# Gate and up products: hi and lo of the activations side by side as one 512-column operand

## The chip, the cores and the metric

The kernel runs on one core of a Trainium2 chip, as one launch. The metric is the device time of that launch in microseconds (us); smaller is better. Engines are named as the profile names them: PE is TensorE (its weight loads are listed apart as PEld), ACT is ScalarE, DVE is VectorE, POOL is GpSimd, and SP issues the transfers.

## The reference, cut to what matters

The program is a two-layer decoder trunk on 256 tokens of 1024 features in float32: four SwiGLU half steps, an attention and convolution mixer between the first and second of them, and an RWKV-7 mixer between the third and fourth. The change is about the half steps:

```python
def macaron_half_ffn(x, pre_g, post_g, w_gate, w_up, w_down):
    h = rmsnorm(x, pre_g)
    h = (jax.nn.silu(h @ w_gate) * (h @ w_up)) @ w_down
    return x + 0.5 * rmsnorm(h, post_g)
```

`w_gate` and `w_up` are 1024 x 2816, `w_down` is 2816 x 1024.

## The kernel before

**Products.** A float32 number is split into two parts, hi and lo, whose sum it is, both of type float32r. A product is three matmuls into one bank of PSUM: hi by hi, hi by lo and lo by hi. `mm3` (L257) issues them, at L260, L261 and L262; its argument `a` is the operand that is loaded as weights (128 x 128), `b` the one that streams past them. `split_u` (L206) makes the two parts of a piece of weights: hi on ACT (L219), lo on DVE, and for every third piece in a half step on POOL (L224).

**Activations.** `norm_in` (L178) allocates two tiles, hi and lo, each of 8 blocks of 128 features by 256 tokens. `pre_norm` scales a tile of 128 tokens, and `hT_split` (L296) transposes it and splits it into the two tiles.

**A half step** (`ffn_body`, L390) has three parts.
- The first 512 of the 2816 columns, in token layout (L402 to L422): the activations are the loaded operand, 512 columns of weights stream.
- The other 2304 columns, transposed (L424 to L439). One round of the loop on `kb` takes 256 columns of gate and 256 of up, 9 rounds in all. Here 128 columns of weights (8 blocks of 128 x 128) are the loaded operand, called a set below, and the 256 tokens stream. A bank holds two sets beside each other, 256 columns each: one `fl` bank for gate, one `mm` bank for up. A set takes 8 calls of `mm3`. Behind a round stand Silu of the gate bank (ACT, L436), its product with the up bank (DVE, L437), and the split of the result into hi and lo (ACT L203, DVE L204). This part is called the wide stage.
- `out_proj` (L329): the product with `w_down`, 512 columns of weights streaming, into two `fl` and two `mm` banks, and behind it the norm and the sum with x.

**Order of work.** Transfers of 1 MB into four `raw` buffers are issued by SP in the order of the program. A set's hi and lo each take one of 18 `u` buffers, so about nine sets of weights can be ready; the split of a set further on waits until PE has finished a set. PSUM has two `fl` banks, four `mm` banks and two for transposes. A scheduler orders the instructions of each engine when the program is built; each engine then runs its own list in order.

Of the kernel before, what the change touches and what calls it, by code (L numbers as in the profile page):

```python
# [15 lines left out]
P = 128  # L16
D = 1024
S = 256
# [11 lines left out]
class Trunk:  # L30
    # out_proj: steps of a tile-1 tail ahead of the next part's first transposes; its last k blocks go by halves
    PIN = 15
    LAST = 4
    # the weight piece behind which the second tile of x is loaded
    LEAD = (0, 4)
    # layer 0: every how many splits Pool takes one
    SHQ = 2
    SH0 = 2
    # order of work for the tensor engine: c compressed branch, f other projections, m masks; a attention, f convolution
    PROJ = "fccfccccfcccmmfcmcfmmffcfcmfmfcmffcfffccmmmmffccc"  # L40
    ATT = "ffafaffafaffaaaafffaafffaafaaafaaafaafffaaafafafaffaffafffaafafafaafffaaafaaaafffffaffaafa"
# [7 lines left out]
    # columns of the forward substitution's groups  # L49
    CA = 6  # L50
    CB = 11
    # beside the substitution: b bonus, t tokens, v values, h g gates, z zeros
    FILL = "vvvz-vvtvvvbvvvhth-vvvvtthvtvtvv-h-vv-h-"
    # behind it: 0-3 chunks, a-d their norms, x y 64 x 64 inverses, A B gains, p q outputs, o the projection
    TAIL = ("vvvgvz0xxvxx0A00gAggsB0eA000aAy1a1y1a1aa1yBy11b1bb2B22b2B2b222ocpocc33cc33p3d/3dooddodqooo"
            "ooooooq")
    # chunks whose squares are summed on DVE; (chunk, half) scaled on ACT; (tile, half) of the outputs on Pool
# [25 lines left out]
    # ---- storage  # L83
# [24 lines left out]
    def behind(self, engine):  # L108
        """what is traced inside goes behind all that is traced so far on engine"""
        traced = self.nc.cur_bb.bb.instructions  # L110
        return self.tc.issue_after(next(i for i in reversed(traced) if i.engine == engine))

    @contextmanager
    def pe_after(self, ins):
        """the matmuls traced inside wait for ins"""
        traced = self.nc.cur_bb.bb.instructions
        n = len(traced)
        yield
        for i in traced[n:]:
            if i.engine == mybir.EngineType.PE:  # L120
                self.tc.add_manual_dep(i, ins.ins.name, mybir.DependencyInfo(
                    mybir.DependencyClass.Sync, mybir.DependencyReason.DATA))

    @contextmanager
    def pe_in_order(self):
        """the matmuls traced inside are issued as they are traced"""
# [11 lines left out]
    def paced(self, main, fill):  # L138
        """fill in step with main, each of its steps behind the instruction that main yields"""
# [5 lines left out]
    def packed(self):  # L145
        """a carver of small pieces out of one tile of a mixer"""
# [22 lines left out]
    def gain_cols(self, name):  # L169
        """a gain by features on partitions, [128, 8], from a small transfer"""  # L170
# [6 lines left out]

    def norm_in(self, gname):  # L178
        """-> (hi, lo, start): start(m) norms token tile m of x, transposes and splits it"""
        hilo = []  # L180

        def start(m, first=False):
            if m < 0:
                hilo.extend([(self.gain_cols if first else self.gain)(gname), self.b8k(F32R), self.b8k(F32R)])
                return
            g, hi, lo = hilo
            if g.shape[1] == KD:
                self.hT_split(self.pre_norm(m), hi, lo, m, g)
            else:
                self.hT_split(self.pre_norm(m, g), hi, lo, m)  # L190
# [10 lines left out]
    # ---- weights: float32 pieces split exactly into hi + lo, both float32r  # L201
# [4 lines left out]
    def split_u(self, src):  # L206
# [3 lines left out]
        if n == 1 and src.shape[2] == 512:  # L210
            # the first weights: every third piece on the two other engines
# [15 lines left out]
    def load_w(self, src, nk, pieces, transfers=1):  # L227
        """src [128, nk, cols]: split in `pieces` pieces along k; per k (hi, lo)"""
# [11 lines left out]
    def cols(self, src, spans):  # L240
        """the given (start, width) column spans of src [128, 8, cols], side by side"""
# [15 lines left out]
    def mm3(self, out, a, b, start, stop):  # L257
        """out += a^T b, a = (hi, lo), b = (hi, lo)"""
# [5 lines left out]
    # ---- norms  # L264
# [23 lines left out]
    def transposed(self, src, n):  # L288
        """n blocks of 128 columns of src -> [128, n, 128] in PSUM"""
# [6 lines left out]
    def hT_split(self, xn, hi, lo, m, g=None):  # L296
        for h in range(2):
            pt = self.transposed(xn[:, h * 512:(h + 1) * 512], 4)
            s = (slice(None), slice(h * 4, h * 4 + 4), slice(m * P, (m + 1) * P))
            if g is None:  # L300
                self.split(pt, hi[s], lo[s])
                continue
            for i in range(4):
                k = h * 4 + i
                s = (slice(None), k, slice(m * P, (m + 1) * P))
                self.nc.scalar.activation(hi[s], pt[:, i, :], AF.Copy, scale=g[:, k:k + 1])
                self.nc.vector.scalar_tensor_tensor(lo[s], pt[:, i, :], g[:, k:k + 1], hi[s].bitcast(F32),
                                                    op0=ALU.mult, op1=ALU.subtract)

    def post_norm(self, m, g, half):  # L310
        """x[m] += c * rmsnorm(y) * g, y coming in two halves"""
# [16 lines left out]
    # ---- x += c * rmsnorm(a^T w): tile 0 ahead of tile 1 from the k block `split` on  # L328
# [56 lines left out]
    # ---- SwiGLU half step  # L385
    def ffn(self, p):
        hilo, start = self.norm_in(p + "_pre_g")
        return start, lambda after: self.ffn_body(p, *hilo[1:], after)

    def ffn_body(self, p, hhi, hlo, after):  # L390
# [5 lines left out]
        def h(k, m):  # L396
            return hhi[:, k, m * P:(m + 1) * P], hlo[:, k, m * P:(m + 1) * P]
# [4 lines left out]
        # first 512 columns in token layout, tile 0 ahead of tile 1  # L402
# [20 lines left out]
        # the others transposed, both tiles at once  # L423
        for kb in range(4, KF, 2):  # L424
            if kb % 8 == 0:
                at.append((self.b8k(F32R), self.b8k(F32R)))
            bg, bu = self.fbank(), self.bank()
            for src, b in ((wg, bg), (wu, bu)):
                raw = self.cols(src, [(kb * P, 2 * P)])
                for i in range(2):  # L430
                    w = self.split_cols(raw, i * P, P)
                    for k in range(KD):
                        self.mm3(b[:, i * S:(i + 1) * S], w[k], (hhi[:, k, :], hlo[:, k, :]), k == 0, k == KD - 1)
            t = self.xn()
            sg, aa = t[:, :512], t[:, 512:]
            nc.scalar.activation(sg, bg, AF.Silu)  # L436
            nc.vector.tensor_mul(aa, bu, sg)  # L437
# [5 lines left out]
    # ---- layer 0 mixer: sparse attention heads beside a gated short convolution  # L443
    def l0_mix(self):
        hilo, start = self.norm_in("l0_mix_pre_g")
        return start, lambda after: self.l0_body(*hilo[1:], after)

    def l0_body(self, hhi, hlo, after):
# [11 lines left out]
        def h(k, m):  # L460
            return hhi[:, k, m * P:(m + 1) * P], hlo[:, k, m * P:(m + 1) * P]

        def hh(k):
            return hhi[:, k, :], hlo[:, k, :]

        def gather(b, pairs):
            """b = sum of the products, in steps of two"""
# [5 lines left out]
        # queries (scaled, transposed, heads r and r + 4 stacked) and values in token layout  # L473
# [12 lines left out]
        kcT = pk(2, NB)   # the two groups beside each other, each in its own rows  # L486
# [5 lines left out]
        # values and gates side by side  # L492
# [31 lines left out]
        # and the gates, 1 + exp(-g)  # L524
# [15 lines left out]
        # distances, ALiBi and masks  # L540
# [18 lines left out]
        # block features: (parity, dim) on partitions, so that 16 products of 128 rows cover a block  # L559
# [79 lines left out]
        def combine(m, i, ob):  # L639
            """oa[m] += gate_i / sum_i * branch output"""  # L640
# [10 lines left out]
        # selected blocks (all of them at these shapes), window (wider than the sequence)  # L651
# [142 lines left out]
    # ---- layer 1 mixer: RWKV-7 in four chunks of 64 tokens  # L794
# [10 lines left out]
    def l1_setup(self, st):  # L805
# [3 lines left out]
        # per-channel vectors as columns  # L809
# [14 lines left out]
        # first halves of the low-rank maps: decay and rate side by side, and the same times mu  # L824
# [10 lines left out]
    def l1_mixin(self, st, out, i, k, t0, n):  # L835
        """out = h + (shifted h - h) * mu_i for channel block k, tokens t0 .. t0 + n"""
# [3 lines left out]
    def l1_vraw(self, st, hh, i):  # L840
        """value weights, columns of half hh, channel blocks 4 i .. 4 i + 3"""
# [26 lines left out]
    def l1_body(self, st, after):  # L868
# [13 lines left out]
        # constants  # L882
        ones = pk(1)
        V.memset(ones, 1.0)
        mask = pk(P)      # strictly later | not earlier, the same for both halves of the rows
# [4 lines left out]
        rst = pk(CH * 65)  # a running sum that starts over every chunk  # L890
        V.memset(rst, 1.0)
        V.memset(rst[:, 0:CH * 65:65], 0.0)
        sel = self.small.tile([P, NC, 16], F32R, name="sel")   # head of a channel
# [18 lines left out]
        # values: token layout, centred per head (the head norm takes the mean out again);  # L912
        # ZV has the chunk's state updates in rows 0..63 and its values in rows 64..127
# [45 lines left out]
        BK = lambda c: gk[c // 4][:, c % 4]     # [128, chunk, b | k]  # L959
        KR = lambda c: kr_[c // 4][:, c % 4]    # [128, chunk, kappa | r]  # L960
# [16 lines left out]
        # low-rank maps, second halves  # L977
# [29 lines left out]
        def mixes():  # L1007
            """the other mixed inputs, a few blocks at a time"""
# [30 lines left out]
        # keys, decays and in-context rates, two heads at a time  # L1039
# [40 lines left out]
        hsp = self.b8(F32R).rearrange("p (a b s) -> p a b s", a=2, b=2)   # odd | even blocks, hi | lo  # L1080
# [12 lines left out]
        def gram(c):  # L1093
            """per head and chunk: (b | k) against (kappa | r), rows the earlier token"""
# [33 lines left out]
        # head sums -> per token: 1 / |k|^2 and the bonus  # L1128
# [23 lines left out]
        def base():  # L1152
            """inverses of the 32 x 32 diagonal blocks of I + diag(rn) A, one block of one head per partition"""
# [10 lines left out]
            # forward substitution in three independent groups of columns  # L1164
# [19 lines left out]
        def spread(g):  # L1184
            """the inverted blocks of chunks 2 g, 2 g + 1 to the rows of their tokens"""
# [9 lines left out]
        def x64(g):  # L1195
            """the corner blocks of the transposed 64 x 64 inverses"""
# [291 lines left out]
```

## Time and profile before

| | us |
|---|---|
| time, three runs | 1176.79, 1180.26, 1182.51 |
| median | 1180.26 |
| profiled execution, span from first to last instruction | 1176.0 |
| PE busy in the span | 1120.0 |
| PE weight loads busy | 994.9 |
| DVE, ACT, POOL busy | 651.8, 553.3, 441.0 |
| wide stage of one half step (four in all) | about 104 |

The page gives the profiled execution by its span alone. The span lies 0.8 us under the lowest of the three times and 4.3 us under their median, so the profiled execution is like the fastest of the runs. Matmuls are pipelined, and a matmul's record lasts longer than the distance to the next one's start; the rate of PE is therefore read from the distances between starts in the timeline, not from the duration of a record. A row of a group ends with the time its engine sat idle before such instructions and what ended that; idle time of an engine that nobody waits for costs nothing.

### The profile page before, as it was taken

What the parts mean: (1) busy time and instruction counts of PE and PEld (TensorE: products, weight loads), DVE (VectorE), ACT (ScalarE), POOL (GpSimd) and SP (SyncE); (2) the same over time, 40 slices, a digit from 0 to 9 for tenths busy, and PEclk for the clock granted to TensorE, in tenths of its full rate; (3) what the DMA queues carried; (4) which work ended last, traced back from release to release, by engine and by line L of the source; (5) the groups of instructions that cost most, each with busy time, mean ns of one, the idle gap of its engine ahead of it and who ended that gap; (6) DMA issues with size and microseconds to landing.
All of it is one profiled execution on the core that took longest, in us unless ns stands there. A gap on an engine that the chain in (4) does not pass through costs nothing. (4 is left out here: it accounts for less than half of the span.)

```text
span 1176.0 us, 18835 instructions
## 1 busy us (share of the span) xinstructions
PE 1120.0 (95%) x7581; PEld 994.9 (85%) x7581; DVE 651.8 (55%) x1021; ACT 553.3 (47%) x962; POOL 441.0 (37%) x400
## 2 busy tenths in 40 slices
PE   7999998998989999998999999988889988999997
PEld 5999986898978999887999988776557866999986
DVE  5543425656876444327543434879883786544431
ACT  6544434245755444435544432557543455544430
POOL 3523233232564323224523343434461654432321
PEclk9999999989999999999999999999996889999999
DMA  9955562542556665545765552532312244855520
GB/s 322 286 179 179 183 206 67 161 144 72 175 174 206 199 200 189 181 145 179 228 202 162 181 179 90 176 113 72 108 44 83 73 138 149 251 180 181 178 108 36
DMA packets 130756, 187.59 MB, mean 160 GB/s; under 512 B 6871, under 2 KB 101087, under 8 KB 130670
## 3 DMA queue, kind: packets, MB, share of 16 engines
q1 hardware_dynamic: 130670, 186.41, 48.9%
q8 instruction: 59, 0.97, 0.3%
q14 instruction: 27, 0.22, 0.1%
HBM read 185.34 MB, written 1.05 MB: 158 GB/s over the span
## 5 line engine op out<-in xcount | busy, mean ns | idle before, releaser
L224 POOL TENSOR_TENSOR u<-raw,u 128x512 fp32r<-128x512 f32 x222 | 317.3, 1451 | 495.9 <-ACT u L219 477.8
L219 ACT ACTIVATE u<-raw 128x1024 fp32r<-128x1024 f32 x312 | 328.1, 1058 | 338.8 <-PE mm L261 162.4
L224 DVE TENSOR_TENSOR u<-raw,u 128x1024 fp32r<-128x1024 f32 x201 | 273.8, 1366 | 267.1 <-ACT u L219 266.6
L260 PE MATMUL fl<-b,u 128*128 128x256 f32 x688 | 198.0, 288 | 0.1
L262 PE MATMUL fl<-b,u 128*128 128x256 f32 x688 | 197.6, 287 | 0.0
L261 PE MATMUL fl<-b,u 128*128 128x256 f32 x688 | 196.6, 286 | 0.0
L261 PE MATMUL mm<-b,u 128*128 128x256 f32 x592 | 167.7, 283 | 0.0
L262 PE MATMUL mm<-b,u 128*128 128x256 f32 x592 | 167.6, 283 | 0.0
L260 PE MATMUL mm<-b,u 128*128 128x256 f32 x592 | 167.6, 283 | 0.0
L260 PEld LDWEIGHTS fl<-b,u 128*128 128x128 f32 x688 | 133.7, 194 | 1.1 <-ACT u L219 0.5
L262 PEld LDWEIGHTS fl<-b,u 128*128 128x128 f32 x688 | 133.6, 194 | 0.8 <-POOL u L224 0.2
L261 PEld LDWEIGHTS fl<-b,u 128*128 128x128 f32 x688 | 133.4, 194 | 0.2
L262 PE MATMUL fl<-u,b 128*128 128x512 f32 (+1 forms) x304 | 119.2, 393 | 3.6 <-DVE b L204 3.3
L260 PE MATMUL fl<-u,b 128*128 128x512 f32 (+1 forms) x304 | 119.7, 395 | 2.6 <-ACT b L203 1.7
L261 PE MATMUL fl<-u,b 128*128 128x512 f32 (+1 forms) x304 | 119.2, 392 | 1.5 <-DVE u L224 1.5
L260 PE MATMUL mm<-u,b 128*128 128x512 f32 (+1 forms) x296 | 114.7, 389 | 0.0
L260 PEld LDWEIGHTS mm<-b,u 128*128 128x128 f32 x592 | 113.8, 192 | 0.2
L261 PEld LDWEIGHTS mm<-b,u 128*128 128x128 f32 x592 | 113.8, 192 | 0.1
L262 PEld LDWEIGHTS mm<-b,u 128*128 128x128 f32 x592 | 113.8, 192 | 0.0
L261 PE MATMUL mm<-u,b 128*128 128x512 f32 (+1 forms) x296 | 113.3, 384 | 0.2 <-DVE u L224 0.2
L262 PE MATMUL mm<-u,b 128*128 128x512 f32 (+1 forms) x296 | 112.6, 382 | 0.0
L262 PEld LDWEIGHTS fl<-u,b 128*128 128x128 f32 x304 | 58.3, 192 | 16.9 <-DVE b L204 4.4
(292 smaller groups left out, 1641.0 us busy)
## 6 DMA issues: line engine op xcount, KB each, us to landing
raw<-in_l_ffn_w_up_dram SPq DMA_DIRECT2D x44, 1024.0 KB, 5.5
raw<-in_l_ffn_w_down_dram SPq DMA_DIRECT2D x44, 1024.0 KB, 4.9
raw<-in_l_ffn_w_gate_dram SPq DMA_DIRECT2D x42, 1024.0 KB, 5.4
raw<-in_l_w_in_dram SPq DMA_DIRECT2D x9, 1024.0 KB, 5.5
raw<-in_l_w_v_dram SPq DMA_DIRECT2D x6, 1024.0 KB
raw<-in_l_w_out_dram SPq DMA_DIRECT2D x4, 1024.0 KB
raw<-in_l_w_r_dram SPq DMA_DIRECT2D x4, 1024.0 KB
raw<-in_l_w_k_dram SPq DMA_DIRECT2D x4, 1024.0 KB, 6.2
```

Of the source, the lines that this page charges most:

```text
L219: self.nc.scalar.activation(hi, src, AF.Copy)
L224: (self.nc.gpsimd if pool else self.nc.vector).tensor_sub(lo[c], src[c], hi[c].bitcast(F32))
L260: mm(out, a[0], b[0], start=start, stop=False)
L261: mm(out, a[0], b[1], start=False, stop=False)
L262: mm(out, a[1], b[0], start=False, stop=stop)
```

## The change

The activations' hi and lo go into two tiles of another layout, each with 4 blocks of features by (hi, lo) by 256 tokens. So for a block of features hi and lo lie beside each other, 512 columns in a row. All users of the activations take their views by the new `hl`; their instructions stay as they were, with other addresses.

In the wide stage a new function `mm_wide` takes the place of eight calls of `mm3`. For each block it streams the 512 columns of hi and lo past the hi weights into a whole bank, and the 256 columns of hi past the lo weights into the bank's first half; the last block has these two in the other order. A set now fills a bank of its own: its first half holds hi by hi and lo by hi, its second half hi by lo. When the bank is read, ACT copies the second half to SBUF and DVE adds the first half to it. Silu and the product read SBUF then. Both raw tiles of a round are fetched at its head, and the sets go gate, up, gate, up in place of gate, gate, up, up.

```diff
+    def hl_tiles(self):
+        return [self.b8(F32R).rearrange("p (k i s) -> p k i s", k=4, i=2) for _ in range(2)]
+    def hl(self, t, k, s=slice(0, S)):
+        return tuple(t[k // 4][:, k % 4, i, s] for i in range(2))
...
+    def mm_wide(self, b, w, t):
+        mm = self.nc.tensor.matmul
+        for k in range(KD):
+            x = t[k // 4][:, k % 4]
+            b2 = b.rearrange("p (i s) -> p i s", i=2)
+            if k < KD - 1:
+                mm(b2, w[k][0], x, start=k == 0, stop=False)
+                mm(b2[:, 0], w[k][1], x[:, 0], start=False, stop=False)
+            else:
+                mm(b2[:, 0], w[k][1], x[:, 0], start=False, stop=False)
+                mm(b2, w[k][0], x, start=False, stop=True)
...
         for kb in range(4, KF, 2):
...
-            bg, bu = self.fbank(), self.bank()
-            for src, b in ((wg, bg), (wu, bu)):
-                raw = self.cols(src, [(kb * P, 2 * P)])
-                for i in range(2):
-                    w = self.split_cols(raw, i * P, P)
-                    for k in range(KD):
-                        self.mm3(b[:, i * S:(i + 1) * S], w[k], (hhi[:, k, :], hlo[:, k, :]), k == 0, k == KD - 1)
+            raws = [self.cols(src, [(kb * P, 2 * P)]) for src in (wg, wu)]
             t = self.xn()
             sg, aa = t[:, :512], t[:, 512:]
-            nc.scalar.activation(sg, bg, AF.Silu)
-            nc.vector.tensor_mul(aa, bu, sg)
+            for i in range(2):
+                for raw, bank, dst in ((raws[0], self.fbank, sg), (raws[1], self.bank, aa)):
+                    b, dst = bank(), dst[:, i * S:(i + 1) * S]
+                    self.mm_wide(b, self.split_cols(raw, i * P, P), ht)
+                    nc.scalar.activation(dst, b[:, S:], AF.Copy)
+                    nc.vector.tensor_add(dst, b[:, :S], dst)
+            nc.scalar.activation(sg, sg, AF.Silu)
+            nc.vector.tensor_mul(aa, aa, sg)
```

Three places show what the built programs make of it. The first is PE's list in the first half step's wide stage, where it passes from one set to the next. In the names `fl` and `mm` are the banks, `b8` the activations, `u` the parts of the weights; `u_428` and `u_457` are hi of two sets, `u_429` and `u_458` lo. Before:

```order
L260 MATMUL mm_367<-b8_102,u_428 128x256
L261 MATMUL mm_367<-b8_103,u_428 128x256
L262 MATMUL mm_367<-b8_102,u_429 128x256
L260 MATMUL mm_367<-b8_102,u_457 128x256
L261 MATMUL mm_367<-b8_103,u_457 128x256
L262 MATMUL mm_367<-b8_102,u_458 128x256
```

The same place in the changed program, where `u_418` and `u_442` are hi of two sets, `u_419` and `u_443` lo:

```order
L404 MATMUL fl_417<-b8_103,u_418 128x512
L405 MATMUL fl_417<-b8_103,u_419 128x256
L407 MATMUL fl_417<-b8_103,u_419 128x256
L408 MATMUL fl_417<-b8_103,u_418 128x512
L404 MATMUL mm_441<-b8_102,u_442 128x512
L405 MATMUL mm_441<-b8_102,u_443 128x256
```

Three matmuls of 256 columns have become two, of 512 and 256 columns, and the bank changes with every set.

The second place is ACT's list in the same stage: splits of weights (`u<-raw`), and between them the work on finished banks. Before:

```order
L219 ACTIVATE u_773<-raw_743 128x1024
L219 ACTIVATE u_803<-raw_801 128x1024
L436 ACTIVATE xn_609<-fl_490 128x512
L219 ACTIVATE u_832<-raw_801 128x1024
L219 ACTIVATE u_869<-raw_867 128x1024
L203 ACTIVATE b8_141<-xn_609 128x512
```

The changed program over one round:

```order
L454 ACTIVATE xn_576<-fl_577 128x256
L211 ACTIVATE b8_141<-xn_472 128x512
L227 ACTIVATE u_830<-raw_777 128x1024
L454 ACTIVATE xn_576<-mm_601 128x256
L227 ACTIVATE u_853<-raw_779 128x1024
L454 ACTIVATE xn_576<-fl_624 128x256
L227 ACTIVATE u_885<-raw_879 128x1024
L456 ACTIVATE xn_576<-xn_576 128x512
L454 ACTIVATE xn_576<-mm_647 128x256
```

A copy out of a bank (L454) now stands between every two splits, and Silu (L456) reads SBUF, behind DVE's sum of the second gate set.

The third place is PE's list where the first half step goes from the wide stage to `out_proj`. There `fl_1505` and `fl_1509` of before are the banks of token tile 0, `mm_1513` and `mm_1517` those of tile 1. Before:

```order
L262 MATMUL mm_1365<-b8_102,u_1456 128x256
L260 MATMUL fl_1505<-u_1497,b8_141 128x512
L261 MATMUL fl_1505<-u_1498,b8_141 128x512
L262 MATMUL fl_1505<-u_1497,b8_142 128x512
L260 MATMUL fl_1509<-u_1497,b8_141 128x512
```

In the changed program `fl_1307`, `mm_1315` and `mm_1319` are three of these four banks:

```order
L408 MATMUL mm_1263<-b8_103,u_1264 128x512
L268 MATMUL fl_1307<-u_1299,b8_141 128x512
L269 MATMUL fl_1307<-u_1300,b8_141 128x512
L270 MATMUL fl_1307<-u_1299,b8_142 128x512
L268 MATMUL mm_1315<-u_1299,b8_141 128x512
```

The products for the second `fl` bank, which the last gate set still holds, come after 19 matmuls of this stage now, where they came after 3: those for the other banks stand ahead of them.

Elsewhere PE's list is the same but for line numbers in the first half step's opening and in the RWKV mixer, and nearly so in the rest; in the attention of layer 0 some heads' and convolution products change places. The list of transfers is the same but for one `w_down` transfer that moves behind six small ones.

More of the change, by code (lines that the diff above doesn't have):

```diff
@@ L183, in start @@
             if m < 0:
-                hilo.extend([(self.gain_cols if first else self.gain)(gname), self.b8k(F32R), self.b8k(F32R)])
+                hilo.extend([(self.gain_cols if first else self.gain)(gname), *self.hl_tiles()])
                 return
-            g, hi, lo = hilo
+            g, *hl = hilo
             if g.shape[1] == KD:
-                self.hT_split(self.pre_norm(m), hi, lo, m, g)
+                self.hT_split(self.pre_norm(m), hl, m, g)
             else:
-                self.hT_split(self.pre_norm(m, g), hi, lo, m)
+                self.hT_split(self.pre_norm(m, g), hl, m)
         return hilo, start
@@ L294, in transposed, with hT_split @@
         return pt[:, :n * P].rearrange("p (a b) -> p a b", b=P)
-    def hT_split(self, xn, hi, lo, m, g=None):
+    def hT_split(self, xn, t, m, g=None):
         for h in range(2):
             pt = self.transposed(xn[:, h * 512:(h + 1) * 512], 4)
-            s = (slice(None), slice(h * 4, h * 4 + 4), slice(m * P, (m + 1) * P))
+            hi, lo = (t[h][:, :, i, m * P:(m + 1) * P] for i in range(2))
             if g is None:
-                self.split(pt, hi[s], lo[s])
+                self.split(pt, hi, lo)
                 continue
@@ L304, in hT_split @@
                 k = h * 4 + i
-                s = (slice(None), k, slice(m * P, (m + 1) * P))
-                self.nc.scalar.activation(hi[s], pt[:, i, :], AF.Copy, scale=g[:, k:k + 1])
-                self.nc.vector.scalar_tensor_tensor(lo[s], pt[:, i, :], g[:, k:k + 1], hi[s].bitcast(F32),
+                self.nc.scalar.activation(hi[:, i], pt[:, i, :], AF.Copy, scale=g[:, k:k + 1])
+                self.nc.vector.scalar_tensor_tensor(lo[:, i], pt[:, i, :], g[:, k:k + 1], hi[:, i].bitcast(F32),
                                                     op0=ALU.mult, op1=ALU.subtract)
@@ L387, in ffn, with ffn_body @@
         hilo, start = self.norm_in(p + "_pre_g")
-        return start, lambda after: self.ffn_body(p, *hilo[1:], after)
-    def ffn_body(self, p, hhi, hlo, after):
+        return start, lambda after: self.ffn_body(p, hilo[1:], after)
+    def mm_wide(self, b, w, t):
[9 more added lines that the diff above has]
+                mm(b2, w[k][0], x, start=False, stop=True)
+    def ffn_body(self, p, ht, after):
         nc = self.nc
@@ L396, in h @@
         def h(k, m):
-            return hhi[:, k, m * P:(m + 1) * P], hlo[:, k, m * P:(m + 1) * P]
+            return self.hl(ht, k, slice(m * P, (m + 1) * P))
         def a(k, m):
@@ L445, in l0_mix, with l0_body @@
         hilo, start = self.norm_in("l0_mix_pre_g")
-        return start, lambda after: self.l0_body(*hilo[1:], after)
-    def l0_body(self, hhi, hlo, after):
+        return start, lambda after: self.l0_body(hilo[1:], after)
+    def l0_body(self, ht, after):
         nc, A = self.nc, self.A
@@ L460, in h @@
         def h(k, m):
-            return hhi[:, k, m * P:(m + 1) * P], hlo[:, k, m * P:(m + 1) * P]
+            return self.hl(ht, k, slice(m * P, (m + 1) * P))
         def hh(k):
-            return hhi[:, k, :], hlo[:, k, :]
+            return self.hl(ht, k)
         def gather(b, pairs):
@@ L1383, in head_out @@
             yield
-            self.hT_split(y, mx[0], mx[1], m)
+            self.hT_split(y, mx, m)
             yield
@@ L1391, in a @@
         def a(k, m):
-            return mx[0][:, k, m * P:(m + 1) * P], mx[1][:, k, m * P:(m + 1) * P]
+            return self.hl(mx, k, slice(m * P, (m + 1) * P))
         def zeros():
@@ L1431, in spread1 @@
             yield
-        mx.extend([self.b8k(F32R), self.b8k(F32R)])
+        mx.extend(self.hl_tiles())
         out = self.out_proj(lambda k: wo[:, k:k + 2, :], a, list(range(KD)), 0, "l1_mix_post_g", False, after, True)
```

## The prediction

> **What bounds the kernel now.** I read the page's first lines, then busy time by stretch, then PE's timeline in the long stretches.
>
> ```profile
> span 1176.0 us, 18835 instructions
> PE 1120.0 (95%) x7581; PEld 994.9 (85%) x7581; DVE 651.8 (55%) x1021; ACT 553.3 (47%) x962; POOL 441.0 (37%) x400
> ```
>
> PE is busy nearly all the time, the others about half. A share over the whole span hides stages, so next come the four wide stages and, in the last row, the attention mixer (columns: length, then busy time and instructions of each engine, granted clock, DMA share, GB/s):
>
> ```profile
> 35.30:139.80 104.50, 104.50 (x873) 104.48 (x872) 46.67 (x45) 48.88 (x57) 34.56 (x26) 1.00 0.64 206
> 374.20:478.30 104.10, 104.10 (x870) 104.06 (x869) 46.01 (x43) 47.18 (x54) 35.83 (x27) 1.00 0.63 200
> 566.60:670.70 104.10, 104.10 (x870) 104.06 (x869) 45.99 (x43) 47.19 (x54) 35.84 (x27) 1.00 0.61 195
> 1006.00:1110.00 104.00, 104.00 (x869) 103.99 (x868) 45.95 (x43) 47.23 (x54) 34.74 (x26) 1.00 0.63 202
> 200.00:374.20 174.20, 163.19 (x1048) 146.01 (x1049) 120.25 (x272) 88.55 (x183) 67.64 (x60) 0.96 0.48 152
> ```
>
> In each wide stage PE never pauses, at full clock, and DVE and ACT are used for under half of it. The splits of weights on ACT show who waits for whom (line L219 within the first wide stage; behind the second bar stands ACT's idle time ahead of them and what ended it):
>
> ```profile
> L219 ACT ACTIVATE u<-raw 128x1024 fp32r<-128x1024 f32 x37 | 39.2, 1060 | 53.5 <-PE mm L261 18.6 <-PE fl L261 15.6 <-PE fl L262 9.7
> ```
>
> They wait for PE to give buffers back, not for transfers. The four stages, 416 us together, are pure PE time, and what the change is worth there is what it takes off PE.
>
> **What a matmul costs there.** The distance between starts counts. PE's timeline in a wide stage (start, length of the record, in us):
>
> ```profile
> 100.01 0.28 PE L261 MATMUL mm<-b,u 128*128 128x256 f32 x1
> 100.13 0.28 PE L262 MATMUL mm<-b,u 128*128 128x256 f32 x1
> 100.25 0.28 PE L260 MATMUL mm<-b,u 128*128 128x256 f32 x1
> 100.37 0.28 PE L261 MATMUL mm<-b,u 128*128 128x256 f32 x1
> ```
>
> A matmul of 256 columns takes 120 ns. The 869 PE records in 104.0 us of the fourth stage give the same, 104.0 / 869 = 119.7 ns. For 512 columns, in an `out_proj`:
>
> ```profile
> 500.06 0.39 PE L260 MATMUL fl<-u,b 128*128 128x512 f32 x1
> 500.29 0.39 PE L261 MATMUL fl<-u,b 128*128 128x512 f32 x1
> 500.52 0.39 PE L262 MATMUL fl<-u,b 128*128 128x512 f32 x1
> 500.75 0.39 PE L260 MATMUL fl<-u,b 128*128 128x512 f32 x1
> ```
>
> And 40 us of nothing but such matmuls, as busy time by stretch:
>
> ```profile
> 680.00:720.00 40.00, 40.00 (x178) 33.13 (x177) 10.50 (x9) 12.94 (x14) 8.26 (x7) 1.00 0.54 174
> ```
>
> Three steps take 0.69 us, 230 ns each in hundredths. The long stretch is finer: 178 records touch it, two of which, at 0.39 us a record, began before it; 40.00 / 176 = 227 ns. So twice the columns cost less than twice the time. A straight line through (256, 120) and (512, 227) has 107 / 256 = 0.418 ns a column and 120 - 107 = 13 ns a matmul. The value projection has matmuls of 280 columns, for which the line gives 13 + 117 = 130 ns:
>
> ```profile
> 212.76 0.29 PE L260 MATMUL fl<-u,b 128*128 128x280 f32 x1
> 212.89 0.29 PE L261 MATMUL fl<-u,b 128*128 128x280 f32 x1
> 213.02 0.29 PE L262 MATMUL fl<-u,b 128*128 128x280 f32 x1
> 213.15 0.29 PE L260 MATMUL fl<-u,b 128*128 128x280 f32 x1
> ```
>
> They start 130 ns apart. So 13 ns belong to the matmul, not to its columns.
>
> **Term 1, the matmuls.** A block's product is 3 x 256 columns before, 3 x 120 = 360 ns. Now it is 512 and 256 columns: the same 768 columns, one matmul and one weight load fewer. What a pair of mixed lengths costs, the ends of the wide stages show:
>
> ```profile
> 374.06 0.39 PE L262 MATMUL mm<-u,b 128*128 128x512 f32 x1
> 374.29 0.28 PE L261 MATMUL fl<-b,u 128*128 128x256 f32 x1
> ...
> 478.16 0.28 PE L262 MATMUL mm<-b,u 128*128 128x256 f32 x1
> 478.28 0.40 PE L260 MATMUL fl<-u,b 128*128 128x512 f32 x1
> 478.51 0.40 PE L261 MATMUL fl<-u,b 128*128 128x512 f32 x1
> ```
>
> 512 then 256 takes 230 ns to the next start, 256 then 512 takes 120: each keeps its own price whatever its neighbour is. I take 227 + 120 = 347 ns, 13 less than 360. There are 4 half steps x 9 rounds x 4 sets x 8 blocks = 1152 blocks, so the term is 1152 x 13 ns = 15.0 us, 3.7 of each wide stage's 104. The bounds: 0, if the 13 ns follow columns in this stage after all; and all three fixed parts gone, if columns alone counted, 39 ns x 1152 = 45 us.
>
> The row first, then a rule against this change: the rows give 13 ns for each matmul. The Trainium skill, page TensorE: Matmul & The Clock Gate, section "Wait — 56ns, not 53.3ns?", has warm matmuls start N / 2.4 + 2.5 ns apart, the 2.5 ns fixed. By that figure a block would save 2.5 ns and the term would be an estimated 2.9 us. The rows here (120 and 227 ns against its 109 and 216) don't agree with it, and I stay with the rows.
>
> **Term 2, reading the banks.** Each of 144 sets gains a copy of 256 columns on ACT and a sum on DVE; each of 36 rounds has its Silu and product read SBUF. The nearest rows for the copy (first two), the sum (third), Silu out of PSUM and a pass of that size out of SBUF, the product with PSUM and a product of SBUF alone:
>
> ```profile
> L1059 ACT ACTIVATE xn<-fl,pk 128x256 f32<-128x256 f32 x16 | 6.8, 472 | 2.9 <-POOL b L1076 2.4 <-DVE b L1091 0.4
> L1027 ACT ACTIVATE b<-mm 128x256 f32<-128x256 f32 x8 | 2.9, 377 | 10.8 <-PE mm L262 10.8
> L1071 DVE TENSOR_TENSOR xn<-mm,xn 128x256 f32<-128x256 f32 x8 | 3.3, 416 | 0.0
> L436 ACT ACTIVATE xn<-fl 128x512 f32<-128x512 f32 x36 | 20.9, 580 | 0.0
> L203 ACT ACTIVATE b<-xn 128x512 fp32r<-128x512 f32 x36 | 22.1, 614 | 0.0
> L437 DVE TENSOR_TENSOR xn<-mm,xn 128x512 f32<-128x512 f32 x36 | 24.9, 692 | 57.9 <-PE mm L262 57.9
> L649 DVE TENSOR_TENSOR u<-u 128x512 f32<-128x512 f32 x4 | 3.9, 965 | 0.0
> ```
>
> The copy is 377 to 472 ns; I take the middle, 0.42 us. In one stage ACT gains 36 x 0.42 + 9 x 0.03 = 15.4 us and DVE 36 x 0.416 + 9 x 0.27 = 17.4 us. That makes 62.6 us of ACT and 63.4 of DVE in a stage of 100: both stay under two thirds. This work lies beside PE and costs nothing, as long as banks come back in time. If that cover went, each set would show its 0.84 us, 144 x 0.84 = 121 us.
>
> **The new wait.** The copy waits for the last matmul of its set; behind it in ACT's list stand the next split and the rest of the round, and behind the sum on DVE the lo parts of later sets. Does anyone wait for those? A split is made about eight sets, 8 x 2.8 = 22 us, before PE needs it, and today it waits for PE at the same moments. The bank: a gate set takes one of two `fl` banks, so it must be read within the three sets that follow, 3 x 8 x 0.347 = 8.3 us. How long reading takes to start today (last gate matmul, the next split, then Silu):
>
> ```profile
> 1035.00 0.28 PE L262 MATMUL fl<-b,u 128*128 128x256 f32 x1
> ...
> 1035.33 1.06 ACT L219 ACTIVATE u<-raw 128x1024 fp32r<-128x1024 f32 x1 [1.90 <-PE fl L262]
> 1036.30 0.58 ACT L436 ACTIVATE xn<-fl 128x512 f32<-128x512 f32 x1
> ```
>
> Silu starts 1.0 us after the set ends at 1035.28, behind one split. With the copy, one more split's delay and the sum it is 1.0 + 1.1 + 0.42 + 0.42 = 2.9 us, against 8.3. The up sets have four banks and more time. At the handover to `out_proj` the second `fl` bank is asked for after one up set and 19 matmuls, 2.8 + 19 x 0.227 = 7.1 us after its gate set. No wait for PE, so 0.
>
> **Term 3, order.** Gate's raw tile is held through the third split of a round instead of the second, one set (2.8 us) longer; with DMA at 61 to 64% in the stages and no split there waiting for a transfer, 0. SP's list keeps its order but for one `w_down` transfer behind six small ones, 0. The attention mixer's products change places a little; PE idles 174.2 - 163.2 = 11.0 us there, and I allow a quarter of that, 3 us, either way, and take 0. The first half step's opening and the RWKV mixer keep PE's order, and the transposes and splits only write other addresses: 0.
>
> **Sum.** 1176.0 - 15.0 = 1161.0 us for the span. The profiled execution lies 4.3 us below the median of the runs; with the same for the new kernel, 1180.3 - 15.0 = 1165.3, and I say **1165 us**.
>
> **Rivals.**
> - *Streams alone count* (faster than forecast). The 13 ns may be weights that are not in place in time; behind 512 columns there is time to fetch them. Then a block takes its columns, 768 x 0.418 = 321 ns, and the kernel 1180.3 - 45 = 1135. For it: loads are busy for all of each stage (104.06 of 104.10 us). Against it: 512-column matmuls, which give a load twice the time, pay the 13 ns too. The Trainium skill, page Trainium Kernel Development and Optimization, Performance Expectations, names load busy time a good measure and matmul busy time a bad one; by that rule a third fewer loads should pay best, and the equal 13 ns of both lengths speak against it. Chance 0.05.
> - *Little or no gain*. Either the fixed part is shared out in another way here, or the 512 columns are run as two passes, so that the change doesn't do what it says: 1177 to 1180; if a fifth of the 13 ns were the matmul's own, the gain would be 3 us and the time 1177. Against it: the 280-column row, which fits 13 ns a matmul, and 512 columns into one bank at 227 ns. The skill's 2.5 ns above would end here. Chance 0.10.
> - *Banks come back late* (slower). ACT and DVE run their lists in order, and Silu now waits on ACT for DVE's sum. If reading a gate set took over 8.3 us, PE would wait at each of the 72 later gate sets; the gain is gone at 15.0 / 72 = 0.21 us, so from 8.5 us on the kernel is slower, and at 9.0 us it would take 1165 + 72 x 0.7 = 1215. For it: the work on ACT and DVE grows by a third. Against it: the 2.9 us above. Chance 0.05.
>
> **How the numbers follow.** The forecast has 0.80. Its own spread is 3 us for the mixer and 3 for the runs (they lie from 3.5 below to 2.3 above their median), 1159 to 1171. The range goes on to take in the second rival, up to 1178, and a fixed part some ns larger than 13 below, 1156; outside lie the two rivals of 0.05 and about 0.05 of the forecast. About 0.5%, 6 us, is what a measurement of this kernel can tell from no change: faster 0.80 + 0.05 = 0.85, same 0.10, slower 0.05.
>
> **What would show it.** In the new profile the starts in a wide stage alternate by 227 and 120 ns, each stage lasts about 100.3 us with PE never idle, ACT and DVE are each near 63 us in it, and the splits on ACT still wait for PE. Pairs of 320 ns would prove the first rival, 360 the second; idle PE ahead of the first matmul of a gate set, ended by DVE, the third. If the stages shorten and the time doesn't, the loss lies in the attention mixer or at the handovers.

## The result and the profile after

The new kernel takes 1170.65 us, the median of four runs (1169.4 to 1172.56); the kernel before takes 1180.2 (1176.79 to 1182.51, four runs). The ratio is 0.9932, with a 95% interval of 0.9913 to 0.9952: faster by 0.7%, which is more than the 0.5% that can be told from no change. The forecast was 1165, with 1156 to 1178 as its range.

The head of the page of the new kernel, in the same columns as before:

```profile
span 1168.7 us, 16781 instructions
PE 1114.8 (95%) x6429; PEld 936.0 (80%) x6429; DVE 706.0 (60%) x1165; ACT 594.7 (51%) x1106; POOL 444.6 (38%) x400
```

There are 7581 - 6429 = 1152 matmuls fewer, one in each block. PE's idle time in the span goes from 1176.0 - 1120.0 = 56.0 us to 53.9, so PE's waits have not grown in all.

The four wide stages of the new kernel, each from the first of its matmuls to the first of `out_proj` (length, then busy time and instructions of PE, PEld, DVE, ACT and POOL, the granted clock, DMA share, GB/s):

```profile
35.96:138.31 102.35, 102.35 (x586) 89.11 (x584) 60.16 (x80) 58.69 (x91) 37.16 (x26) 1.00 0.64 212
370.71:472.62 101.91, 101.91 (x582) 88.73 (x581) 57.71 (x78) 57.22 (x90) 37.27 (x27) 1.00 0.62 207
562.50:664.54 102.04, 102.04 (x582) 88.64 (x580) 57.88 (x78) 57.31 (x90) 37.35 (x27) 1.00 0.62 202
1000.80:1102.72 101.92, 101.92 (x581) 88.69 (x580) 57.85 (x78) 56.80 (x89) 35.85 (x26) 1.00 0.61 203
```

The same stages, cut the same way, took 104.54, 103.99, 103.99 and 103.98 us before; the last of them reads

```profile
1006.01:1109.99 103.98, 103.98 (x868) 103.98 (x867) 45.94 (x43) 47.22 (x54) 34.73 (x26) 1.00 0.63 202
```

PE never pauses in either kernel, and the clock is the same. But a stage has become 2.1 us shorter, where the forecast had 3.7: 416.50 - 408.22 = 8.3 us in all instead of 15.0. What lies between the stages takes 1.0 us more (1168.7 - 408.2 against 1176.0 - 416.5), within the 3 us allowed for that.

PE's timeline in a wide stage of the new kernel (start, length of the record) shows the place where the forecast is off:

```profile
99.87 0.40 PE L404 MATMUL fl<-b,u 128*128 128x512 f32 x1
100.11 0.28 PE L405 MATMUL fl<-b,u 128*128 128x256 f32 x1
100.23 0.40 PE L404 MATMUL fl<-b,u 128*128 128x512 f32 x1
100.47 0.28 PE L405 MATMUL fl<-b,u 128*128 128x256 f32 x1
100.58 0.40 PE L404 MATMUL fl<-b,u 128*128 128x512 f32 x1
100.81 0.28 PE L405 MATMUL fl<-b,u 128*128 128x256 f32 x1
100.93 0.40 PE L404 MATMUL fl<-b,u 128*128 128x512 f32 x1
```

Three pairs take 100.93 - 99.87 = 1.06 us, 353 ns a pair; the forecast had 347. By the nanoseconds of the trace the time from a 512's start to the next start goes round in three steps, about 233, 236 and 241 ns, and that from a 256's start in 113, 117 and 120. The 1008 matmuls of L404 average 235.6 ns, the 1008 of L405 116.9. Alone they are 227 and 120. So a pair costs some 6 ns more than its two parts, and over 1152 blocks that is the 7 us that are missing from the wide stages.

### The profile page after: what moved, and what is told of

Read it like the earlier page. It is cut to its first block, busy times and chain, and to the rows that moved or that the text cites. A ratio compares the mean times of both kernels' runs of the same rounds, so it can differ in the third digit from the quotient of the medians.

```text
span 1168.7 us, 16781 instructions
## 1 busy us (share of the span) xinstructions
PE 1114.8 (95%) x6429; PEld 936.0 (80%) x6429; DVE 706.0 (60%) x1165; ACT 594.7 (51%) x1106; POOL 444.6 (38%) x400
## 5 line engine op out<-in xcount | busy, mean ns | idle before, releaser
L232 POOL TENSOR_TENSOR u<-raw,u 128x512 fp32r<-128x512 f32 x222 | 322.1, 1472 | 485.3 <-ACT u L227 478.3
L232 DVE TENSOR_TENSOR u<-raw,u 128x1024 fp32r<-128x1024 f32 x201 | 277.0, 1383 | 211.8 <-ACT u L227 211.4
L404 PE MATMUL mm<-b,u 128*128 128x512 f32 x504 | 181.3, 398 | 0.0
L404 PE MATMUL fl<-b,u 128*128 128x512 f32 x504 | 180.7, 397 | 0.0
L405 PE MATMUL fl<-b,u 128*128 128x256 f32 x504 | 141.5, 281 | 0.0
L405 PE MATMUL mm<-b,u 128*128 128x256 f32 x504 | 141.4, 280 | 0.0
L404 PEld LDWEIGHTS fl<-b,u 128*128 128x128 f32 x504 | 94.9, 188 | 19.6
L404 PEld LDWEIGHTS mm<-b,u 128*128 128x128 f32 x504 | 94.8, 188 | 19.7
L405 PEld LDWEIGHTS mm<-b,u 128*128 128x128 f32 x504 | 95.2, 189 | 3.4
L405 PEld LDWEIGHTS fl<-b,u 128*128 128x128 f32 x504 | 95.2, 189 | 3.1
L268 PEld LDWEIGHTS fl<-u,b 128*128 128x128 f32 x304 | 58.9, 194 | 16.4 <-ACT b L211 1.9
L270 PEld LDWEIGHTS fl<-u,b 128*128 128x128 f32 x304 | 58.2, 192 | 17.0 <-DVE b L212 3.5
L269 PEld LDWEIGHTS fl<-u,b 128*128 128x128 f32 x304 | 58.5, 193 | 13.1 <-DVE u L232 1.7
L268 PEld LDWEIGHTS mm<-u,b 128*128 128x128 f32 (+1 forms) x296 | 56.0, 190 | 12.1 <-issue 0.8
L269 PEld LDWEIGHTS mm<-u,b 128*128 128x128 f32 (+1 forms) x296 | 56.0, 190 | 11.2 <-DVE u L232 0.6
```

Of the source, the lines that this page charges most:

```text
L232: (self.nc.gpsimd if pool else self.nc.vector).tensor_sub(lo[c], src[c], hi[c].bitcast(F32))
L268: mm(out, a[0], b[0], start=start, stop=False)
L269: mm(out, a[0], b[1], start=False, stop=False)
L270: mm(out, a[1], b[0], start=False, stop=stop)
L404: mm(b2, w[k][0], x, start=k == 0, stop=False)
L405: mm(b2[:, 0], w[k][1], x[:, 0], start=False, stop=False)
```

## The experiments

The first four ask what makes a pair dearer; the other five ask what that depends on, and whether it can be had back.

**Three matmuls again.** Layout, banks, reading of banks and order of sets stay as in the change; only the 512 columns are streamed as two times 256, and the last block of a set has no order of its own.

```diff
-            if k < KD - 1:
-                mm(b2, w[k][0], x, start=k == 0, stop=False)
-                mm(b2[:, 0], w[k][1], x[:, 0], start=False, stop=False)
...
+            mm(b2[:, 0], w[k][0], x[:, 0], start=k == 0, stop=False)
+            mm(b2[:, 1], w[k][0], x[:, 1], start=False, stop=False)
+            mm(b2[:, 0], w[k][1], x[:, 0], start=False, stop=k == KD - 1)
```

> This kernel has everything of the change (side-by-side layout, a bank per set, copy and sum, order of sets) but three matmuls of 256 columns per block again. Theory A, the whole gain comes from the matmuls and reading the banks is free: wide stages of 104.0 us as before, time 1180 within 3 us. Theory B, a part of the missing gain is lost to reading the banks or to the new order: the wide stages stay at 104 but the other stages grow, time 1181 to 1185.

It takes 1179.38 us against 1179.74 for the kernel before, ratio 0.9995 (0.9985 to 1.0005). The fourth wide stage of this kernel:

```profile
1005.24:1109.23 103.99, 103.99 (x869) 103.98 (x867) 59.10 (x78) 56.74 (x88) 35.67 (x26) 1.00 0.60 202
```

The stage is as long as before (103.98), although ACT and DVE do the added work (56.74 and 59.10 us). All else that the change brings costs and gains nothing that these runs can tell; the gain comes from the matmuls.

**Lengths grouped in a set.** The same matmuls as the change, but for each set first the eight of 512 columns, then the eight of 256.

```diff
+        b2 = b.rearrange("p (i s) -> p i s", i=2)
         for k in range(KD):
...
+            mm(b2, w[k][0], t[k // 4][:, k % 4], start=k == 0, stop=False)
+        for k in range(KD):
+            mm(b2[:, 0], w[k][1], t[k // 4][:, k % 4, 0], start=False, stop=k == KD - 1)
```

> The same sums, but in each set first the eight 512-column matmuls, then the eight 256-column ones. In the changed kernel a block takes 353 ns instead of 347. Theory M, it is the alternation of two lengths that costs the 6 ns: slots of 227 and 120 ns, a set 2776 ns instead of 2823, each wide stage 100.3 us, time about 1164. Theory O, a 512-column matmul costs about 235 ns with these operands whoever its neighbour is: slots of 235 and 120, stages of 102 us or a little more, time 1170 to 1172.

It takes 1166.95 us (1165.34 to 1168.45, four runs), ratio to before 0.9888 (0.9869 to 0.9907); the intervals of this ratio and of the change's do not meet. Its fourth stage:

```profile
999.20:1100.17 100.97, 100.97 (x581) 88.90 (x580) 58.06 (x78) 57.54 (x89) 35.89 (x26) 1.00 0.62 205
```

The same matmuls, weights and columns in another order take 0.95 us less than in the change. Here the 512s average 230.4 ns and the 256s 119.2, 349.6 together. So the order of lengths costs time, and somewhat more than half of what was missing is regained.

**The lo weights stream 512 columns too.** All matmuls of the stage have one length. This kernel computes lo by lo as well, which neither kernel does.

```diff
-            if k < KD - 1:
-                mm(b2, w[k][0], x, start=k == 0, stop=False)
-                mm(b2[:, 0], w[k][1], x[:, 0], start=False, stop=False)
...
+            mm(b2, w[k][0], x, start=k == 0, stop=False)
+            mm(b2, w[k][1], x, start=False, stop=k == KD - 1)
```

> The lo weights stream all 512 columns too (this adds lo by lo), so all matmuls of the stage have one length. Theory M: no alternation, slots of 227 ns, a set 16 x 227 = 3632 ns, each stage 130.8 us. Theory O: slots of 235 ns, a set 3760 ns, each stage 135.4 us.

One run took 1288.65 us. Its fourth stage, and three starts in its first:

```profile
1089.87:1220.91 131.04, 131.04 (x582) 108.54 (x580) 59.82 (x78) 58.11 (x89) 35.69 (x26) 1.00 0.48 158
```

```profile
99.74 0.39 PE L404 MATMUL mm<-b,u 128*128 128x512 f32 x1
99.97 0.39 PE L403 MATMUL mm<-b,u 128*128 128x512 f32 x1
100.20 0.39 PE L404 MATMUL mm<-b,u 128*128 128x512 f32 x1
```

131.04 us are 576 x 227 ns and 0.3 us. A 512 in this stage, with these weights, these banks and ACT and DVE at work beside it, takes 227 ns if its neighbours are as long. So the 235 ns don't belong to the operands of this stage.

**PE alone.** A kernel of stretches of 48 blocks, with resident tiles and nothing else running; it computes no part of the reference. The stretches differ in one thing each.

```diff
+        for g in range(G):  # B: the pair
+            b = banks[g % 4]
+            for k in K:
+                mm(b, w(0, k), x5(k), **S_(k))
+                mm(b[:, :256], w(1, k), x2(k), **E_(k))
```

> No part of the reference is computed; PE alone works, on resident tiles, in 15 stretches of one pattern each, 48 blocks a stretch, with the other engines and the queues idle. Theory C, the other engines' work on the same memory costs the 6 ns: the pair (stretch B) takes 347 ns here. Theory M: B 353, 512 alone (C) 227, 512 and 512 of two weights (L) 227 each, grouped (E) 227 and 120. Theory O: B 353, C and L near 235, while 512 with weights from the activations' tile and the stream from a weight tile (D, as in the output projection) stays at 227. Three of 256 (A) 360 by all.

Six of its stretches, by busy time: three matmuls of 256; the pair; 512 alone; grouped by eight; the pair with the 256 into another bank; the pair with the same weights twice.

```profile
29.11:46.39 17.28, 17.28 (x147) 17.28 (x146) 0.00 (x0) 0.00 (x0) 0.00 (x0) 1.00 0.00 1
46.39:63.35 16.96, 16.96 (x99) 14.72 (x97) 0.00 (x0) 0.00 (x0) 0.00 (x0) 1.00 0.00 1
63.35:74.25 10.90, 10.90 (x50) 9.01 (x49) 0.00 (x0) 0.00 (x0) 0.00 (x0) 1.00 0.00 0
85.13:101.87 16.74, 16.74 (x98) 14.75 (x97) 0.00 (x0) 0.00 (x0) 0.00 (x0) 1.00 0.00 1
101.87:118.83 16.96, 16.96 (x99) 14.70 (x97) 0.00 (x0) 0.00 (x0) 0.00 (x0) 1.00 0.00 1
118.83:135.79 16.96, 16.96 (x99) 14.70 (x97) 0.00 (x0) 0.00 (x0) 0.00 (x0) 1.00 0.00 1
```

By 48 blocks that is 360, 353.3, 227.1, 348.7, 353.3 and 353.3 ns. The pair has its 353 ns with ACT, DVE, POOL and DMA idle, whatever the bank and the weights; with the 256 from another tile or from the second half, or with all operands in weight tiles, it is 353 again (16.95 to 16.96 us for 48 blocks). The cost belongs to the sequence of lengths on PE and to nothing around it.

**How long the runs of one length are.** PE alone again, 64 matmuls of each length in a stretch, in runs of 1, 2, 4, 8, 16 and 32; then other lengths. No part of the reference is computed here either.

```diff
+            for _ in range(n // r):
+                for _ in range(r):
+                    one(0, n1)
+                for _ in range(r if n2 else 0):
+                    one(1, n2)
```

> PE alone on resident tiles; no part of the reference is computed. 64 matmuls of each length per stretch, in runs of 1, 2, 4, 8, 16 and 32 of 512 and then as many of 256 columns; then 512, 256, 384 and 320 alone; then single alternation of 512/384, 384/256, 320/256, 512/320. Theory M1 (each change of length costs 3.3 ns, whatever the run): 353.4, 350.2, 348.6, 347.7, 347.2, 347.0 ns for a 512 and a 256 together. Theory M2 (the extra belongs to the first few matmuls behind a change, up to about five, so it first stays and then falls): 353.4, 353, 351, 348.6, 347.8, 347.4. Both: 384 alone 173 and 320 alone 147 ns by the line of 13.3 + 0.417 a column. Alternations: if any change of length costs the same, 407, 300, 273 and 380 ns; if only the step of 512 against 256 does, 400, 293, 267 and 373 (the sums).

The six runs of 512 and 256, then 384/256 and 512/320 in single alternation:

```profile
29.73:52.34 22.61, 22.61 (x131) 19.60 (x129) 0.00 (x0) 0.00 (x0) 0.00 (x0) 1.00 0.00 1
52.34:74.65 22.31, 22.31 (x131) 19.46 (x129) 0.00 (x0) 0.00 (x0) 0.00 (x0) 1.00 0.00 1
74.65:97.10 22.45, 22.45 (x130) 19.61 (x129) 0.00 (x0) 0.00 (x0) 0.00 (x0) 1.00 0.00 1
97.10:119.45 22.35, 22.35 (x131) 19.66 (x129) 0.00 (x0) 0.00 (x0) 0.00 (x0) 1.00 0.00 1
119.45:141.71 22.26, 22.26 (x130) 19.67 (x129) 0.00 (x0) 0.00 (x0) 0.00 (x0) 1.00 0.00 1
141.71:163.94 22.23, 22.23 (x130) 19.69 (x129) 0.00 (x0) 0.00 (x0) 0.00 (x0) 1.00 0.00 1
...
232.65:251.43 18.78, 18.78 (x129) 18.78 (x129) 0.00 (x0) 0.00 (x0) 0.00 (x0) 1.00 0.00 1
...
268.49:292.67 24.18, 24.18 (x130) 21.56 (x128) 0.00 (x0) 0.00 (x0) 0.00 (x0) 1.00 0.00 1
```

By 64, a 512 and a 256 take 353.3, 348.6, 350.8, 349.2, 347.9 and 347.3 ns. Neither M1 (353.4, 350.2, 348.6, 347.7) nor M2 (353.4, 353, 351, 348.6) fits: runs of two are cheaper than runs of four or eight. By the nanoseconds, in long runs the first five 512s behind 256s take 233, 236, 228, 233 and 231 ns and then 227, and the first 256 behind 512s takes 114, the others 119 or 120. For runs of eight and more this gives a plain estimate: a return from 256 to 512 costs 26 ns on five 512s (1161 against 5 x 227) and gives back 6 on a 256, some 20 ns a round. Eights then come to 347.0 + 20 / 8 = 349.5 ns and sixteens to 348.3, where 349.2 and 347.9 were measured. Shorter runs don't follow it: it would give 352 ns for runs of four and 357 for runs of two.

The single alternation of 384 and 256 takes 18.78 / 64 = 293.4 ns, the sum of its parts (173.4 and 119.9), and 320/256 also its sum; 512/320 takes 377.7, 4 ns above its sum of 373.6, and 512/384 406.7, 6 above 400.5.

**Runs of two in the kernel.** For each pair of blocks two 512s, then two 256s.

```diff
-        for k in range(KD):
...
+        for k0 in range(0, KD, 2):
+            for k in (k0, k0 + 1):
+                mm(b2, w[k][0], t[k // 4][:, k % 4], start=k == 0, stop=False)
+            for k in (k0, k0 + 1):
+                mm(b2[:, 0], w[k][1], t[k // 4][:, k % 4, 0], start=False, stop=k == KD - 1)
```

> The change, with two 512s and then two 256s per pair of blocks: half as many changes of length, nothing else. Theory M1 (3.3 ns a change): blocks of 350 ns, 288 x 3.3 = 1.0 us off each wide stage, about 101.1 us each, and about 1166.8 us. Theory M2 (the first few behind a change pay, so short runs pay as much each): blocks near 353, stages near 102, and about 1170.5 us.

It takes 1166.33 us (1164.38 to 1167.78, five runs), ratio 0.9887 (0.9869 to 0.9904). Its fourth stage:

```profile
999.28:1100.06 100.78, 100.78 (x582) 87.99 (x580) 57.86 (x78) 56.76 (x88) 35.90 (x26) 1.00 0.62 205
```

100.8 us, under both expectations (101.1 and 102), with 233.3 and 115.5 ns, 348.8 a pair: what the runs of two of PE alone had given (348.6).

**The grouped order once more**, beside the two others on one chip; the kernel is that of the second experiment.

> The grouped order (eight 512s, then eight 256s in a set) once more, beside the two others on one chip: 1167 us and wide stages of 101.0 us, as in its first run, by either theory.

1166.78 us (1166.12 to 1169.55, six runs), ratio 0.9901 (0.9885 to 0.9917), stages of 101.43, 100.99, 101.07 and 100.95: as in its first run.

**Two sets together.** A gate and an up set take their banks together: sixteen 512s, then sixteen 256s; reading the two banks follows.

```diff
-    def mm_wide(self, b, w, t):
+    def mm_wide(self, sets, t):
...
+        for b, w in sets:
+            for k in range(KD):
+                mm(b.rearrange("p (i s) -> p i s", i=2), w[k][0], t[k // 4][:, k % 4], start=k == 0, stop=False)
+        for b, w in sets:
+            for k in range(KD):
+                mm(b[:, :S], w[k][1], t[k // 4][:, k % 4, 0], start=False, stop=k == KD - 1)
...
```

> A gate and an up set together: sixteen 512s, then sixteen 256s, in two banks. Half as many changes as the grouped order. Both theories: the grouped order's excess of some 20 ns a set halves, 36 x 10 ns = 0.4 us off each stage, 100.6 us, and about 1165.5 us, a little faster than the grouped order. Rival: the excess of the grouped order belongs to the start of a bank, not to the change of length; then stages stay at 101.0 and the time at 1167. Second rival: two banks are released together and late, PE waits ahead of gate sets, and it is slower than the grouped order by some us.

It takes 1166.09 us (1163.86 to 1168.87, five runs), ratio 0.989 (0.9871 to 0.9908). Its fourth stage:

```profile
997.01:1097.62 100.61, 100.61 (x582) 89.00 (x581) 59.84 (x78) 57.32 (x89) 35.68 (x26) 1.00 0.63 206
```

The stage is 0.34 us shorter than with sets apart (100.95), as both theories had it: an excess at the start of each bank would have left it at 101.0. PE never waits for a bank. The times of this kernel, of the runs of two and of the grouped order lie within each other's runs, and which of the three is best can't be told by time. All three are faster than the kernel before. The change was not run beside them: by ratio to the kernel before, the interval of the grouped order just reaches that of the change (0.9913), and those of the other two don't. The wide stages of all three are shorter than the change's (402.9 to 404.4 us against 408.2).

**Which lengths pay.** PE alone, 64 of each in single alternation: 416, 448, 480 and 496 columns alone, these with 256, and five other pairs. No part of the reference is computed.

```diff
-        alt(512, 256, 1)
+        alt(416, 0, 1)
...
+        alt(448, 256, 1)
+        alt(512, 448, 1)
```

> PE alone on resident tiles, no part of the reference is computed: 416, 448, 480 and 496 columns alone, then single alternation of each with 256, then 512/448, 512/480, 448/384, 480/384 and 256/128, 64 of each. Alone, by 13.3 + 0.417 a column: 186.7, 200.0, 213.3 and 220.0 ns. Theory L1 (only a matmul of 512 columns, a full bank, pays when its neighbour is shorter): the pairs with 416 to 496 take their sums, 306.6, 319.9, 333.2 and 339.9 ns; 512/448 and 512/480 take 6 ns more than their sums of 427 and 440; 448/384 and 480/384 take 373 and 387. Theory L2 (the extra comes where weight loads no longer fill the time, that is for streams longer than the 188 ns of a load's record, from about 420 columns on): nothing at 416, and an extra that grows to 6 ns from 448 to 496; 448/384 and 480/384 pay as well. 256/128 tells whether short pairs ever pay: 120 and 66.7 ns alone, 186.5 by either.

Alone at 448; then 448/256, 496/256 and 512/448:

```profile
40.41:53.37 12.96, 12.96 (x65) 12.02 (x64) 0.00 (x0) 0.00 (x0) 0.00 (x0) 1.00 0.00 1
...
101.16:121.66 20.50, 20.50 (x130) 19.52 (x129) 0.00 (x0) 0.00 (x0) 0.00 (x0) 1.00 0.00 1
...
142.99:164.75 21.76, 21.76 (x130) 19.52 (x129) 0.00 (x0) 0.00 (x0) 0.00 (x0) 1.00 0.00 1
164.75:192.76 28.01, 28.01 (x130) 24.04 (x129) 0.00 (x0) 0.00 (x0) 0.00 (x0) 1.00 0.00 1
```

448 alone takes 202.6 ns, 2.6 above the line, and 416, 480 and 496 lie 1.8, 3.3 and 3.3 above it; alternated with 256 all four take the sum by the line (320.4 against 320.0 at 448, 340.0 against 340.0 at 496). Over the line 512/448 costs 11 ns extra, 512/480 7, and 448/384 and 480/384 6.6 each. Over their parts as measured alone that is 8.0, 3.1, 4.0 and 3.2 ns, and the four pairs with 256 lie 1.7 to 3.3 ns below theirs. By either measure L1 falls (448/384 costs extra without a 512), and so does L2 (448/256 to 496/256 cost nothing extra). 256/128 took 229.6 ns against 186.5; 128 alone was not tried, so that says nothing of alternation.

## Why the prediction was right, and where it was off

The time lies in the range and on the side that had 0.85, and the mechanism is the one named. The price of mixed lengths was mis-sized. That the time stayed within the forecast's own spread, 1159 to 1171, is partly luck: that spread stood for the mixer and the runs, and the prediction gave the mixed pair no allowance.

**What bounds the kernel: right.** Take the sum of the four wide stages of each kernel's profile from its median time:

| kernel | wide stages, us | time, us | rest, us |
|---|---|---|---|
| before | 416.5 | 1180.2 | 763.7 |
| the change | 408.2 | 1170.65 | 762.4 |
| three matmuls again | 416.6 | 1179.38 | 762.8 |
| grouped in a set (second time) | 404.4 | 1166.78 | 762.3 |
| runs of two | 403.6 | 1166.33 | 762.7 |
| two sets together | 402.9 | 1166.09 | 763.2 |
| lo weights with 512 | 524.7 | 1288.65 (one run) | 763.9 |

The rest stays within 1.6 us while the stages go over nearly 122. What PE takes in these stages is what the kernel takes. And PE alone gives the stages: 1152 blocks at the price measured with PE alone, and the 1.8 us that the kernel before has beyond 1152 x 360 ns, come to 408.8 us for single alternation, 404.1 for runs of eight, 403.4 for runs of two and 402.6 for runs of sixteen; measured were 408.2, 404.4, 403.6 and 402.9.

**13 ns for each matmul: right.** The lengths of 320 and 384 columns, which were not in the line, lie on it: 146.5 and 173.4 ns measured, 146.7 and 173.4 by 13.3 + 0.417 a column. The other price that stood beside it, the 2.5 ns of the Trainium skill, page TensorE: Matmul & The Clock Gate, section "Wait — 56ns, not 53.3ns?", would have given an estimated 2.9 us; the stages gained 8.3, and 13.6 with two sets together (416.5 - 402.9). These traces disagree with it for matmuls that each bring their own weights in float32r.

**The failed step of Term 1: "each keeps its own price whatever its neighbour is".** It was read off two single changes of length at the ends of stages, in a timeline of 0.01 us, and the whole term is 13 ns a block. Two roundings can hide what such a pair costs: 6.3 ns more than its parts in single alternation (353.3 ns with PE alone, 353 in the kernel). Besides, the step took the price of the last matmul ahead of each change, and what a change costs shows behind it. The kernel before has this too, where `out_proj` follows the 256s:

```profile
478.28 0.40 PE L260 MATMUL fl<-u,b 128*128 128x512 f32 x1
478.51 0.40 PE L261 MATMUL fl<-u,b 128*128 128x512 f32 x1
478.75 0.39 PE L262 MATMUL fl<-u,b 128*128 128x512 f32 x1
478.97 0.40 PE L260 MATMUL fl<-u,b 128*128 128x512 f32 x1
479.21 0.39 PE L261 MATMUL fl<-u,b 128*128 128x512 f32 x1
479.44 0.39 PE L262 MATMUL fl<-u,b 128*128 128x512 f32 x1
```

The first five 512s take 479.44 - 478.28 = 1.16 us, where 5 x 227 ns is 1.135; by the nanoseconds they take 235, 235, 228, 232 and 231. In single alternation a block gains not 13 ns but 6.7, and the term is 1152 x 6.7 = 7.7 us instead of 15.0; the stages show 8.3. The step gave no bound of its own for the mixed pair; the 10 ns that a timeline of two decimals leaves open on each change would have been one. That the sum by 347 ns was to be had is shown by runs of sixteen and thirty-two (347.9 and 347.3 ns).

**Term 2, reading the banks: right.** The kernel with three matmuls, at 1179.38 us against 1179.74, shows no cost. The added and changed operations in the new kernel, as groups over the whole span:

```profile
L454 ACT ACTIVATE xn<-mm 128x256 f32<-128x256 f32 x72 | 26.3, 365 | 0.0
L455 DVE TENSOR_TENSOR xn<-mm,xn 128x256 f32<-128x256 f32 x72 | 30.1, 418 | 35.0 <-ACT xn L454 35.0
L456 ACT ACTIVATE xn<-xn 128x512 f32<-128x512 f32 x36 | 22.3, 620 | 6.1 <-DVE xn L455 6.1
L457 DVE TENSOR_TENSOR xn<-xn 128x512 f32<-128x512 f32 x36 | 24.9, 693 | 1.2
```

The copy takes 365 ns where 420 was taken, under both its rows; the sum 418 (416), Silu 620 (614). The product takes 693, as it did with a bank, not the 965 of the row that was chosen: an overcharge of 0.27 us a round that hid in slack. ACT is busy for 57 to 59 us of a stage and DVE for 58 to 60; 63 was forecast.

**The new wait: right.** The end of a gate set in the new kernel, the split and the copy behind it, and the sum:

```profile
1026.35 0.40 PE L408 MATMUL fl<-b,u 128*128 128x512 f32 x1
1026.55 1.06 ACT L227 ACTIVATE u<-raw 128x1024 fp32r<-128x1024 f32 x1 [1.49 <-PE fl L407]
1027.52 0.36 ACT L454 ACTIVATE xn<-fl 128x256 f32<-128x256 f32 x1
1028.78 0.42 DVE L455 TENSOR_TENSOR xn<-fl,xn 128x256 f32<-128x256 f32 x1
```

The set's last matmul hands over at 1026.35 + 0.24 = 1026.59, and the bank has been read at 1029.20: 2.6 us, forecast 2.9, against 8.3 allowed. Over all 72 gate sets it is 2.5 us in the mean and 4.7 at most. The split still waits 1.49 us for PE to give a weight tile back, and not for a transfer.

**Term 3, order: right within its 3 us.** The rest of the table above is 1.3 us smaller after than before, the rest of the profiled spans 1.0 larger; both are within the spread of runs.

**The two medians.** The profiled execution of the new kernel has a span of 1168.7 us and took 1170.47, so 1.8 us lie around the span. It is near its median, where that of before was at the fast end; so the medians differ by 9.55 us and the spans by 7.3. The wide stages, which hardly vary, say 8.3.

**The rivals.** Streams alone count: no, no pair is near 321 ns. Little or no gain: no, but half the term was gone, by a cause that none of the rivals had. Banks late: no, PE has no idle time in a wide stage.

**What stays open** is the rule behind the extra. Shown: it depends on PE's sequence of lengths alone; it isn't a price per change (runs of two beat runs of four and eight) nor one of 512 columns as such; of the single alternations with 256 whose parts were measured only that with 512 costs extra. Nothing of PE's inside was seen that explains this.

## What to carry to other kernels

Where PE is never idle, fewer and longer matmuls can gain the fixed part of each, here 13 ns, but measure the sequence that will run: a short kernel of PE alone gave the wide stages of the four orders in the kernel to within 0.6 us of some 400. If products of two lengths must mix, try runs of two or sort them by length within a bank: here the same matmuls in these orders took some 4 us less. When a term is a dozen nanoseconds times a thousand, a timeline rounded to 10 ns is too coarse to settle it; take the mean over a long stretch of just that sequence, or put the rounding into the range.

## What the hardware showed that was not expected

Alternating 512 and 256 columns costs 353.3 ns a pair against 347.0 for its parts, in a pattern that repeats every three pairs. Streams of 416 to 496 columns on their own take 1.8 to 3.3 ns more than the line through 256, 320, 384 and 512, but not when a 256 stands between them. And the weight loads' busy time was no measure of the time here: it fell from 103.98 to 88.69 us in the fourth stage with a third fewer loads, while the stage fell by 2%.
